# A streaming encoder layer in one planned stream: second home for z tiles, free PSUM positions from one list, state decay as a step of its own

## The chip, the cores and the metric

One Trainium2 chip, one of its cores. The metric is the device time of one execution in microseconds, from launch to end. The profiled execution has besides a span, from its first to its last instruction.

## The reference, cut to what matters

One layer for 2048 prompt rows and 64 sample rows, model width 1024. The input projection has 10,272 columns; a Mamba-2 branch works in chunks over 8 groups of 4 heads, a pooling branch beside it, then two branch projections, a merge and an output projection.

```python
n = rmsnorm(x, norm_g)
z, xbc, dt_raw, u, pool_gate, gate_logits = split(n @ w_in)
xs, bs, cs = split(silu(causal_dwconv(xbc_ext)))
# ssd_chunk, one chunk:
y_diag = einsum('blgsr,bsgrp->blgrp', CB[..., None] * L, xdt)
y_off  = einsum('blgn,bgrpn->blgrp', C, h) * exp(acum)
h_new  = h * exp(acum[:, -1]) + einsum('blgn,blgrp->bgrpn', B, xdt * decay_end)
# behind the scan:
yf = (y + d_skip * xs) * silu(z)
yg = yf * rsqrt(mean(yf * yf, over the 256 columns of a group) + EPS)
out = (sigmoid(g_a) * (yg @ w_branch_ssd) + sigmoid(g_b) * pool_branch) @ w_out
```

## The kernel before, in words

The rows are handled in three parts of 704 (the third has 640 prompt rows and the 64 sample rows). All large products are done in float32 split into a high and a low half, three matmuls for one product, and the input projection uses seven products in place of eight for a pair of 128-column blocks (a Strassen scheme, class `Pair`, products numbered 1 to 7).

The program of a part is a list of items in `Stream`. An item is one product of 12 matmuls (128x352) that reads one weight slot of eight; the slot is split up to five items ahead by ScalarE (high half, L170) and VectorE (low half, L231). `stream.at(position, step)` puts any other step ahead of the item at that position, and `stream.later(k, step)` puts it k items behind the one where it is called. So the position table in `add_part` decides where each step stands on each engine. TensorE, and after the start ScalarE too, run in exactly this program order; VectorE and the DMA queue of SyncE (SP) are ordered by the tile scheduler along it, and each engine runs its own list in order.

The pairs of a part come in this order: u and pool gate, then merge gates `g`, then for each of 8 groups the pairs `x`, `bc` and `z`. While these products run, the scan of the group before is threaded through them, six units to a group (`unit_load`, `unit_mask`, `unit_exp`, `unit_front`, `unit_back`):

- `unit_front` transposes x and B into the PSUM bank `tp` and forms C·B there; VectorE makes `xdt`, `xdtd` and the masked `bA` of it (L847 to L850).
- `unit_back` makes y in bank `y` and the new state in bank `st`. GpSimd (POOL) decays the state `h` in place (L887) once the y matmuls have read it, then VectorE adds the product (L892). `eB` holds the decay of y, loaded by ScalarE's DMA queue.
- In the third part the sixth unit has the sample rows: its state `hsr` is loaded, turned by TensorE in bank `st` and copied to `hs` by ScalarE, all at the head of `unit_front`.
- Behind a group's last unit come `group_post` (times silu(z), then a DMA of the result to `y_d`), `group_square`, and twice `group_sum` (split of half of the sum of squares into `sqr`) and `group_rms` (two matmuls with ones into the bank `e`).

The bank `e` (one buffer) belongs to product 2 of each pair; the list `quiet` has the positions between, where it is free. `zt` and `sa` have one buffer each, for all z tiles but the last and for all merge gate tiles. Each `group_rms` of the second half is followed by a chain: DMA to `s2_d`, DMA back, VectorE, POOL power, DMA to `rs_d`. In the first part the split slots of x, bc and u are also stored to DRAM (L327), and the other parts load them.

Of the kernel before, what the change touches and what calls it, by code (L numbers as in the profile page):

```python
# [19 lines left out]
NG = 8  # L20
# [110 lines left out]
def kernel(  # L131
# [152 lines left out]
    class Pair:  # L284
# [10 lines left out]
        def early(self, i):  # L295

            if self.stored():
                return ()
            return {1: ((9, 1, self.load0),), 6: ((10, 1, self.load1), (7, 0, self.sums)),
                    3: ((12, 0, self.sum4),)}.get(i, ())  # L300

        def load0(self):
            self.r0 = cols(w_in, pair_cols[self.key][0])
# [248 lines left out]
    def add_part(qi, q):  # L552
# [221 lines left out]
        def z_pair(g):  # L774
            st = grp[g]

            def open_(t):
                if "zt" not in st:
                    if g + 1 < NG:
                        st["zt"] = nm["pc"].tile([P, 2, T], F32, tag="zt", name="zt", bufs=1)  # L780
                    else:
                        st["zt"] = nm["pc"].tile([P, 2, XW], F32, tag="xx", name="zt", bufs=4)[:, :, 0:T]
# [42 lines left out]
        def unit_front(u):  # L825
            g, ci = divmod(u, NC)
            kind, r0, lt, L, xp = q.chunks[ci]
            pc, un, st = nm["pc"], units[u], grp[g]
            xx, bc, bA = st["xx"], st["bc"], un["bA"]
            xs = slice(xp, xp + L)  # L830
            if kind == "s":
                hs = st["hs"] = pc.tile([P, 256], F32, tag="hs", name="hs", bufs=1)
                ps = tpsum("st")
                for t in range(2):
                    transpose(ps[:, t * P:(t + 1) * P], st["hsr"][:, t, :], ident)
                S.copy(out=hs, in_=ps[:, 0:256])
# [13 lines left out]
            V.tensor_tensor(out=bA[0:L, :, 0:L], in0=bA[0:L, :, 0:L],  # L850
                            in1=cb.unsqueeze(1).broadcast_to([L, HPG, L]), op=ALU.mult)
# [7 lines left out]
                dma_a(eB[hh * 64:(hh + 1) * 64, :, 0:L], src.unsqueeze(0).broadcast_to([64, 2, L]))  # L859

        def sample_load(g):
            hsr = grp[g]["hsr"] = nm["pc"].tile([P, 2, P], F32, tag="hsr", name="hsr", bufs=1)
            dma(hsr, state_ssd[0, 0, 4 * g:4 * g + 4].rearrange("(t h) p n -> (h p) t n", t=2))

        def unit_back(u):
            g, ci = divmod(u, NC)
# [17 lines left out]
            if kind == "p":  # L884
                sp = tpsum("st")
                mm(sp[:, 0:256], lhsT=un["bt"][0:L], rhs=un["xdtd"][0:L], start=True, stop=True)
            G.tensor_tensor(out=hd(hcur), in0=hd(hcur),  # L887
                            in1=q.dec[:, ci, 4 * g:4 * g + 4].unsqueeze(2).broadcast_to([P, HPG, 64]), op=ALU.mult)
            yv = st["yt"][:, :, lt:lt + L]
            V.tensor_tensor(out=yv, in0=yb[:, 1, :, 0:L], in1=eB[:, :, 0:L], op=ALU.mult)  # L890
            V.tensor_tensor(out=yv, in0=yb[:, 0, :, 0:L], in1=yv, op=ALU.add)
            V.tensor_tensor(out=hcur, in0=sp[:, 0:256], in1=hcur, op=ALU.add)  # L892

        def group_post(g):
            st = grp[g]
            xx, yt, zt = st["xx"], st["yt"], st["zt"]
            for t0, sl, sg in q.segs:
                for j in range(2):
                    V.scalar_tensor_tensor(out=yt[:, j, t0:t0 + sl], in0=xx[:, j, t0 + sg:t0 + sg + sl],
                                           scalar=dcol[:, 2 * g + j:2 * g + j + 1], in1=yt[:, j, t0:t0 + sl],  # L900
                                           op0=ALU.mult, op1=ALU.add)
            V.tensor_tensor(out=yt, in0=yt, in1=zt, op=ALU.mult)
            dma(y_d[g], yt)
            if not q.last:
                dma(h_d[g], st["h"])
# [12 lines left out]
        def group_rms(g, h):  # L918
            pc, zt, sqr = nm["pc"], grp[g]["zt"], grp[g]["sqr"]
            srow = zt[:, 1]  # L920
            ps = bank("e") if g + 1 < NG else any_tpsum()
            for i in range(2):
                mm(ps[0:32, 0:H], lhsT=onesr, rhs=sqr[:, i], start=i == 0, stop=i == 1)
            S.copy(out=srow[0:1, h * H:(h + 1) * H], in_=ps[0:1, 0:H])
            if not h:
                return
            dma(s2_d[g:g + 1], srow[0:1])
            sc4 = pc.tile([P, 16], F32, tag="sc4", name="sc4")[0:64, 0:NB]
            dma(sc4, s2_d[g].rearrange("(p f) -> p f", f=NB))
            V.tensor_scalar(out=sc4, in0=sc4, scalar1=1.0 / 256, scalar2=EPS, op0=ALU.mult, op1=ALU.add)  # L930
            G.tensor_tensor(out=sc4, in0=sc4, in1=mhalf[0:64, 0:NB], op=ALU.pow)
            dma(rs_d[g].rearrange("(p f) -> p f", f=NB), sc4)
# [65 lines left out]
        quiet = sorted([after[n, 6] for n in range(len(pairs))] + [after[n, 5] for n in range(len(pairs))])  # L998
        before = lambda u, x: slots[u - 1] + x * (slots[u] - slots[u - 1]) if u > 0 else slots[0] - 3.5 * (1 - u - x)
        for u in range(NG * NC + 1):  # L1000
            g, ci = divmod(u, NC)
            if u < NG * NC:
# [1 line left out]
                stream.at(before(u, 0.15), lambda u=u: unit_mask(u))  # L1004
                stream.at(before(u, 0.5), lambda u=u: unit_exp(u))
                stream.at(slots[u], lambda u=u: unit_front(u))
                stream.at(before(u + 1, 0.2), lambda u=u: decay_load(u))
                if q.ns and ci == 3:
                    stream.at(slots[u], lambda g=g: sample_load(g))
            if u:  # L1010
                stream.at(slots[u], lambda u=u: unit_back(u - 1))
            if u and ci == 0:
                g -= 1
                p = max(slots[u], ready("z", g) + 1.5) + 0.01
                if g + 1 < NG:
                    r0, r1, t0, t1 = [t for t in quiet if t >= p + 4.4][0:4]
                else:
                    t0, t1, r0, r1 = p + 1.5, p + 3, p + 4.5, p + 6.5
                stream.at(p, lambda g=g: group_post(g))
                stream.at(p + 2, lambda g=g: group_square(g))  # L1020
                stream.at(p + 3.2, lambda g=g: group_sum(g, 0))
                stream.at(r0, lambda g=g: group_rms(g, 0))
                stream.at(r0 + 0.1, lambda g=g: group_sum(g, 1))
                stream.at(r1, lambda g=g: group_rms(g, 1))
                if q.last:
                    stream.at(t0, lambda g=g: group_state(g, grp[g]["hs"], ssd_s, "e3"))
                    stream.at(t1, lambda g=g: group_state(g, grp[g]["h"], ssd_p, "e1"))
# [340 lines left out]
```

## Time and profile before

| | |
|---|---|
| three runs | 3227.84, 3229.19, 3238.91 us; median 3229.19 us |
| profiled execution | 3231.66 us, span 3229.6 us |
| TensorE (PE) busy | 2958.2 us, 92% of the span |
| VectorE (DVE), ScalarE (ACT), GpSimd (POOL) busy | 1961.9, 1467.8, 829.0 us |
| mean granted TensorE clock | 0.955 of full speed |

The profiled execution lies 2.47 us over the median. PE is the engine with least idle time, so what counts is where PE stands still, and at which clock it runs behind that.

### The profile page before, as it was taken

The numbers are of one execution on the slowest core, as the hardware profiler recorded it, in microseconds if no ns is written. First come the engines' busy times: TensorE is split into PE (matmuls) and PEld (weight loads), VectorE is DVE, ScalarE is ACT, GpSimd is POOL, SyncE is SP. The second block draws the span as 40 slices with busy tenths as digits, with TensorE's granted clock in tenths as the row PEclk, the third lists the DMA queues.
The fourth block names the chain that finished last, engine by engine and source line by source line (L and its number), as shares of the span: only waits on it lengthen the run. The fifth ranks groups of instructions, "written<-read, shape, count | busy, mean of one in ns | idle before, by whom it ended". The sixth has DMA issues, their size and how long they took to land.

```text
span 3229.6 us, 50452 instructions
## 1 busy us (share of the span) xinstructions
PE 2958.2 (92%) x18794; PEld 2827.3 (88%) x18794; DVE 1961.9 (61%) x3462; ACT 1467.8 (45%) x2896; POOL 829.0 (26%) x996
## 2 busy tenths in 40 slices
PE   6999898988899999999899889999999889887998
PEld 6998787878899999998888889999998878887998
DVE  7776767776654556665666665365665566665522
ACT  5445555555442433454544543243345545463411
POOL 4344433433200022322332410012232223341000
PEclk9999998889999999999999999999999999998999
DMA  5566665654586655676565466455567655545734
GB/s 174 180 206 180 216 182 180 223 182 112 198 257 215 211 183 183 198 217 180 158 190 151 103 229 206 148 189 168 189 177 219 177 163 167 151 115 189 230 104 147
DMA packets 502057, 585.07 MB, mean 181 GB/s; under 512 B 43461, under 2 KB 399133, under 8 KB 501813
## 3 DMA queue, kind: packets, MB, share of 16 engines
q1 hardware_dynamic: 390453, 531.50, 49.9%
q10 hardware_dynamic: 111360, 50.36, 8.0%
q8 instruction: 148, 2.42, 0.3%
q14 instruction: 96, 0.79, 0.1%
HBM read 434.31 MB, written 147.44 MB: 180 GB/s over the span
## 4 chain that ended last, share of the span: by engine, by line
PE 37%; DVE 7%; DMA 6%; ACT 4%; issue 2%; POOL 1%; ACTq 1%; SPq 0%; DVEq 0%; POOLq 0%
PE ps_a L183 15%; PE ps_d L183 10%; PE ps_e L183 5%; PE ps_y L183 3%; PE ps_st L183 2%; DVE xx L762 1%; DMA y_d<-yt 1%; DMA bA<-ac_d 1%; PE ps_tp L186 1%; PE ps_tp L183 1%; DVE w L231 1%; DMA wraw<-y_d 1%; DMA g_d<-sa 1%; DMA gt<-g_d 1%; ACT xx L174 1%
## 5 line engine op out<-in xcount | busy, mean ns | idle before, releaser
L183 PE MATMUL ps_a<-N,w 128*128 128x352 f32 x5760 | 998.2, 328 | 30.3 <-ACT e L170 26.2
L183 PEld LDWEIGHTS ps_a<-N,w 128*128 128x128 f32 x5760 | 950.2, 192 | 40.3 <-ACT e L170 32.6
L183 PE MATMUL ps_d<-N,w 128*128 128x352 f32 x2880 | 525.5, 340 | 6.8 <-DVE sa L353 6.8
L183 PEld LDWEIGHTS ps_d<-N,w 128*128 128x128 f32 x2880 | 498.5, 201 | 18.5 <-DVE sa L353 7.3
L231 DVE TENSOR_TENSOR w<-wraw,w 128x512 fp32r<-128x512 f32 x544 | 423.3, 793 | 122.8 <-ACT w L170 120.3
L170 ACT CAST w<-wraw 128x512 fp32r<-128x512 f32 x544 | 326.9, 616 | 158.9 <-POOL wraw L180 61.9
L180 POOL TENSOR_TENSOR S<-wraw 128x512 f32<-128x512 f32 x160 | 232.6, 1454 | 328.2 <-DVE w L231 172.7
L170 ACT COPY e<-ps_a 128x352 f32<-128x352 f32 x360 | 160.4, 448 | 286.1 <-PE ps_a L183 253.3
L183 PE MATMUL ps_e<-N,w 128*128 128x352 f32 x1440 | 273.2, 341 | 8.5 <-DVE ue L353 3.3
L183 PEld LDWEIGHTS ps_e<-N,w 128*128 128x128 f32 x1440 | 247.3, 197 | 14.4 <-DVE sa L353 3.7
L180 POOL TENSOR_TENSOR wraw<-wraw 128x512 f32<-128x512 f32 x160 | 234.0, 1462 | 92.2 <-DVE w L231 83.6
L815 POOL TENSOR_SCALAR_AFFINE_SELECT bA<-bA 128x512 f32<-128x512 f32 x144 | 104.8, 728 | 471.0 <-DMA bA<-ac_d 427.0
L174 ACT ACTIVATE bA<-bA,acum 128x128 f32<-128x128 f32 (+1 forms) x576 | 178.7, 381 | 26.6 <-issue 7.6
L762 DVE SCALAR_TENSOR_TENSOR bc<-raw,cwT,bc 128x704 f32<-128x704 f32 (+1 forms) x144 | 150.4, 1044 | 55.5 <-ACT bc L174 53.8
L762 DVE SCALAR_TENSOR_TENSOR xx<-raw,cwT,xx 128x704 f32<-128x704 f32 (+1 forms) x144 | 154.8, 1075 | 40.4 <-ACT xx L174 39.3
L174 ACT ACT_TABLE_LOAD x105 | 134.7, 1283 | 58.3 <-DVE zt L353 40.3
L892 DVE TENSOR_TENSOR h<-ps_st,h 128x256 f32<-128x256 f32 x136 | 57.1, 420 | 162.8 <-POOL h L887 140.4
L231 DVE TENSOR_TENSOR w<-S,w 128x512 fp32r<-128x512 f32 x176 | 122.0, 696 | 47.9 <-ACT w L170 47.9
L417 POOL TENSOR_TENSOR ss<-ss,mhalf 128x1 f32<-128x1 f32 (+1 forms) x18 | 10.7, 598 | 531.9 <-DVE ss L415 531.9
L183 PE MATMUL ps_d<-yn,w 128*128 128x352 f32 x798 | 131.7, 322 | 0.6 <-DVE w L231 0.2
L183 PE MATMUL ps_a<-yn,w 128*128 128x352 f32 x798 | 130.8, 322 | 0.1
L183 PEld LDWEIGHTS ps_d<-yn,w 128*128 128x128 f32 x798 | 127.8, 188 | 1.9 <-DVE w L231 1.3
(334 smaller groups left out, 4754.5 us busy)
## 6 DMA issues: line engine op xcount, KB each, us to landing
wraw<-in_w_in_dram SPq DMA_DIRECT2D x160, 512.0 KB
w<-wc_x SPq DMA_DIRECT2D x112, 512.0 KB
w<-wc_bc SPq DMA_DIRECT2D x112, 512.0 KB
bA<-ac_d ACTq DMA_DIRECT2D x120, 256.0 KB
wc_x<-w SPq DMA_DIRECT2D x56, 512.0 KB
wc_bc<-w SPq DMA_DIRECT2D x56, 512.0 KB
w<-wc_u SPq DMA_DIRECT2D x56, 512.0 KB
wraw<-in_w_branch_ssd_dram SPq DMA_DIRECT2D x48, 512.0 KB
```

The costliest lines, as they stand in the source:

```text
L170: S.pin(nc.scalar.copy(**k))
L174: S.pin(nc.scalar.activation(*a, **k))
L180: tc.keep_in_program_order(G.tensor_tensor(**k))
L183: tc.keep_in_program_order(nc.tensor.matmul(*a, **k))
L186: tc.keep_in_program_order(nc.tensor.transpose(*a))
L231: V.tensor_tensor(out=dst_lo, in0=src, in1=dst_hi.bitcast(F32), op=ALU.subtract)
L417: G.tensor_tensor(out=ss[0:L, 2:3], in0=ss[0:L, 1:2], in1=mhalf[0:L, 0:1], op=ALU.pow)
L762: V.scalar_tensor_tensor(out=xx[:, i, 0:XL], in0=raw[:, t:t + XL], scalar=cwT[:, t, ct:ct + 1], in1=xx[:, i, 0:XL], op0=ALU.mult, op1=ALU.add)
L815: G.affine_select(out=bA[0:L, :, 0:L], in_=bA[0:L, :, 0:L], compare_op=ALU.is_ge, fill=-1e30, base=0, pattern=[[0, HPG], [1, L]], channel_ ...
L892: V.tensor_tensor(out=hcur, in0=sp[:, 0:256], in1=hcur, op=ALU.add)
```

## The change

- `z` tiles take turns between two homes: even groups in `zt`, odd groups in the merge gates' tile `sa`, the last group as before. The pair of merge gate 3 moves from group 4 to group 5, so that no z tile and gate meet in `sa`. Where two gate pairs follow each other (the last three), the first finishes (products 4 and 3) before product 2 of the next.
- `group_post` writes its product into `zt` itself, the DMA to `y_d` reads `zt`, and `group_square` squares `zt` in place.
- All uses of bank `e` between products draw from one list (`free_bank` takes a position out). The two halves of the mean square now have their `group_sum` two items or more ahead of `group_rms`, and 4 to 7 items between the halves.
- The decayed state is formed ahead by `unit_decay` into a tile `hd`, pinned in POOL's order; `unit_back` only adds.
- The sample state is loaded into a buffer of `eB` and turned by its own step `sample_turn`, in bank `e`.
- Units start one item later (7 for 6 behind the bc pair), the last group's six units take 15 items for 18, `decay_load` comes 0.6 of a unit earlier, `group_square` one item later.
- DMAs of the chain behind the mean square, of `y_d`, `h_d` and of the weight store are issued some items later.

```diff
             if wd is not None:
-                dma(wd[:, i - 1], flat_slot(s))
+                stream.later(2, lambda: dma(wd[:, i - 1], flat_slot(s)))
...
+                    if g + 1 == NG:
+                        st["zt"] = nm["pc"].tile([P, 2, XW], F32, tag="xx", name="zt", bufs=4)[:, :, 0:T]
+                    elif g % 2:
+                        st["zt"] = nm["sg"].tile([P, 2, T], F32, tag="sa", name="zt", bufs=1)
+                    else:
                         st["zt"] = nm["pc"].tile([P, 2, T], F32, tag="zt", name="zt", bufs=1)
...
-            if kind == "s":
-                hs = st["hs"] = pc.tile([P, 256], F32, tag="hs", name="hs", bufs=1)
-                ps = tpsum("st")
-                for t in range(2):
-                    transpose(ps[:, t * P:(t + 1) * P], st["hsr"][:, t, :], ident)
-                S.copy(out=hs, in_=ps[:, 0:256])
...
+        def unit_decay(u):
+            g, ci = divmod(u, NC)
+            h = grp[g]["h" if q.chunks[ci][0] == "p" else "hs"]
+            t = units[u]["hd"] = nm["pc"].tile([P, 256], F32, tag="hd", name="hd", bufs=1)
+            tc.keep_in_program_order(G.tensor_tensor(
+                out=hd(t), in0=hd(h), in1=q.dec[:, ci, 4 * g:4 * g + 4].unsqueeze(2).broadcast_to([P, HPG, 64]),
+                op=ALU.mult))
...
+        def sample_turn(g):
...
+            ps = bank("e") if g + 1 < NG else any_tpsum()
...
-            G.tensor_tensor(out=hd(hcur), in0=hd(hcur),
-                            in1=q.dec[:, ci, 4 * g:4 * g + 4].unsqueeze(2).broadcast_to([P, HPG, 64]), op=ALU.mult)
...
-            V.tensor_tensor(out=hcur, in0=sp[:, 0:256], in1=hcur, op=ALU.add)
+            V.tensor_tensor(out=hcur, in0=sp[:, 0:256], in1=un["hd"], op=ALU.add)
...
-            V.tensor_tensor(out=yt, in0=yt, in1=zt, op=ALU.mult)
-            dma(y_d[g], yt)
+            V.tensor_tensor(out=zt, in0=yt, in1=zt, op=ALU.mult)
+            stream.later(1.5, lambda: dma(y_d[g], zt))
...
-            S.activation(zt, grp[g]["yt"], AF.Square)
+            S.activation(zt, zt, AF.Square)
...
+            stream.later(1, lambda: dma(s2_d[g:g + 1], srow[0:1]))
+            stream.later(2.5, lambda: dma(sc4, s2_d[g].rearrange("(p f) -> p f", f=NB)))
+            stream.later(4, power)
+            stream.later(6, lambda: dma(rs_d[g].rearrange("(p f) -> p f", f=NB), sc4))
...
-            seq += [(n, 6), (n - 1, 3), (n, 5), (n, 7), (n + 1, 1), (n + 1, 2), (n, 4)]
+            seq += [(n, 6), (n - 1, 3), (n, 5), (n, 7), (n + 1, 1)]
+            same = n + 1 < len(pairs) and pairs[n].key[0] == pairs[n + 1].key[0] == "g"
+            seq += [(n, 4), (n, 3), (n + 1, 2)] if same else [(n + 1, 2), (n, 4)]
...
-        S0 = [ready("bc", g) + 6 for g in range(NG)]
-        S0.append(S0[-1] + 18)
+        S0 = [ready("bc", g) + 7 for g in range(NG)]
+        S0.append(S0[-1] + 15)
...
-                stream.at(before(u + 1, 0.2), lambda u=u: decay_load(u))
+                t = before(u, 0.6)
...
+                stream.at(before(u + 1, 0.45), lambda u=u: unit_decay(u))
...
-                    r0, r1, t0, t1 = [t for t in quiet if t >= p + 4.4][0:4]
+                    r0 = free_bank(p + (6 if g in (3, 5, 6) else 10))
+                    r1 = free_bank(r0 + 4)
...
-                stream.at(p + 2, lambda g=g: group_square(g))
-                stream.at(p + 3.2, lambda g=g: group_sum(g, 0))
+                stream.at(p + 3, lambda g=g: group_square(g))
+                stream.at(r0 - 2, lambda g=g: group_sum(g, 0))
```

What this moves, at three places. First ScalarE behind the z pair of group 0 in the first part, before: the square (`zt<-yt`), the split of the first half (`sqr`), and the copy that takes its sum out of bank `e` (`zt<-ps_e`).

```order
L170 CAST w<-S 128x512
L174 ACTIVATE zt<-yt 128x1408
L170 COPY bt<-ps_tp 128x128
L170 CAST w<-wraw 128x512
L170 COPY sa<-ps_a 128x11x32
L177 DMA eB<-eac_d 64x2x128 x2
L170 CAST sqr<-zt 128x352
L170 CAST w<-wraw 128x512
L170 COPY e_3319<-ps_a 128x352
L177 DMA bA<-ac_d 128x4x128
L170 COPY zt<-ps_e 1x352
```

The same queue in the change; the square (`zt<-zt`) stands 13 rows ahead of the first of these rows, directly behind `sa<-ps_a`.

```order
L170 COPY bt<-ps_tp 128x128
L170 CAST w<-S 128x512
L170 CAST sqr<-zt 128x352
L170 CAST w<-wraw 128x512
L170 COPY raw<-ps_a 128x11x32
L174 ACTIVATE xx<-raw,colT,cwT 128x704
L177 DMA bA<-ac_d 128x4x128
L174 ACTIVATE bA<-bA,acum 128x128 x4
L170 CAST w<-wraw 128x512
L170 COPY e_3516<-ps_a 128x352
L177 DMA eB<-eac_d 64x2x128 x2
L170 COPY zt<-ps_e 1x352
```

The square has moved behind the copy out of `ps_a`, and between the split and the copy out of `ps_e` stand eight rows where three stood.

Second TensorE at the sample unit of group 0 in the third part, before: the turn of the sample state (`hsr`) in bank `st`, and the matmul that needs this bank again.

```order
L183 MATMUL ps_d<-N,w 128x352 x24
L183 MATMUL ps_a<-N,w 128x352 x24
L186 MATMUL ps_st<-ident,hsr 128x128 x2
L186 MATMUL ps_tp<-ident,xx 64x128 x2
L186 MATMUL ps_tp<-ident,bc 64x128
L183 MATMUL ps_tp<-bc 64x64
L183 MATMUL ps_y<-bA,xdt 64x128 x4
L183 MATMUL ps_y<-bc,h 128x128 x2
L183 MATMUL ps_st<-xdtd,bt 128x256
```

And in the change:

```order
L183 MATMUL ps_d<-N,w 128x352 x12
L186 MATMUL ps_e<-ident,hsr 128x128 x2
L183 MATMUL ps_a<-N,w 128x352 x24
L183 MATMUL ps_e<-N,w 128x352 x12
L186 MATMUL ps_tp<-ident,xx 64x128 x2
L186 MATMUL ps_tp<-ident,bc 64x128
L183 MATMUL ps_tp<-bc 64x64
L183 MATMUL ps_y<-bA,xdt 64x128 x4
L183 MATMUL ps_y<-bc,h 128x128 x2
L183 MATMUL ps_st<-xdtd,bt 128x256
```

The turn has left bank `st` for bank `e`, whose next user is product 2, two products on (`x24` are two products).

Third POOL in the first part, where units of group 1 run, before: the sums for the weight factors (`S`, `wraw`), the mask of a unit (`bA`) and the decay of the state in place.

```order
L180 TENSOR_TENSOR wraw<-wraw 128x512
L887 TENSOR_TENSOR h<-h,dec 128x256
L815 AFFINE_SELECT bA<-bA 128x512
L180 TENSOR_TENSOR S<-wraw 128x512
L887 TENSOR_TENSOR h<-h,dec 128x256
L764 COPY hcar<-raw 128x3
```

And in the change:

```order
L180 TENSOR_TENSOR wraw<-wraw 128x512 x2
L817 AFFINE_SELECT bA<-bA 128x512
L866 TENSOR_TENSOR hd<-h,dec 128x256
L180 TENSOR_TENSOR S<-wraw 128x512
L764 COPY hcar<-raw 128x3
L817 AFFINE_SELECT bA<-bA 128x512
```

The decay is still one instruction for each unit, but it reads `h` and writes `hd`, so it waits for the state before it and no longer for the matmuls that read it.

## Rows read from the trace of the kernel before

**Rows 1.** The page, section 1: busy us, share of the span, instructions of each engine

```profile
PE 2958.2 (92%) x18794; PEld 2827.3 (88%) x18794; DVE 1961.9 (61%) x3462; ACT 1467.8 (45%) x2896; POOL 829.0 (26%) x996
```

**Rows 2.** Busy us by stretch: PE, PEld, DVE, ACT, POOL; granted clock; DMA share, GB/s

```profile
240.00:860.00 620.00, 541.36 (x3315) 503.48 (x3314) 432.72 (x726) 341.14 (x675) 256.12 (x272) 0.92 0.58 180
860.00:1340.00 480.00, 466.89 (x3046) 458.89 (x3045) 266.21 (x476) 187.08 (x362) 51.15 (x66) 0.99 0.67 217
1340.00:1880.00 540.00, 496.46 (x3164) 462.13 (x3163) 350.17 (x604) 279.18 (x558) 175.52 (x210) 0.95 0.55 164
...
2390.00:2950.00 560.00, 493.19 (x3116) 462.05 (x3114) 345.37 (x638) 283.90 (x580) 175.74 (x250) 0.93 0.55 161
```

**Rows 3.** PE's waits over the span: total us, times, longest us

```profile
PE ps_e L183 <- DVE sqr L231: 42.4, 31, 3.2
PE ps_e L183 <- ACT sqr L170: 29.6, 20, 5.6
PE ps_tp L186 <- ACT bc L174: 27.1, 13, 4.0
...
PE ps_st L183 <- ACT hs L170: 25.1, 5, 6.1
PE ps_tp L186 <- DVE bA L850: 17.0, 9, 4.7
PE ps_y L183 <- DVE yt L891: 12.0, 5, 4.3
PE ps_st L183 <- ACT sqr L170: 8.2, 2, 7.7
```

**Rows 4.** Timeline of PE behind group 0 of part one: start, duration, idle before

```profile
334.99 0.35 PE L183 MATMUL ps_e<-sqr,onesr 128*32 128x352 f32 x1 [2.17 <-ACT sqr L170]
338.17 0.50 PE L183 MATMUL ps_e<-sqr,onesr 128*32 128x352 f32 x1 [2.83 <-DVE sqr L231]
338.47 6.31 PE L183 MATMUL ps_d<-N,w 128*128 128x352 f32 x24
...
352.89 3.98 PE L183 MATMUL ps_a<-N,w 128*128 128x352 f32 x24
```

**Rows 5.** Line 887, the state's decay: ns min/median/max; who waited for it

```profile
L887 POOL TENSOR_TENSOR h<-h,dec x136: 605/615/2086, 271.0 to 2897.9; 128x256 f32<-128x256 f32 x136
...
DVE h L892: 140.4, 57
```

**Rows 6.** A DVE split beside POOL's sums (timeline), and all such splits (line 231)

```profile
337.82 3.13 POOL L180 TENSOR_TENSOR wraw<-wraw 128x512 f32<-128x512 f32 x2
338.04 1.76 DVE L231 TENSOR_TENSOR w<-wraw,w 128x512 fp32r<-128x512 f32 x1
...
L231 DVE TENSOR_TENSOR w<-wraw,w x544: 627/685/2855, 14.9 to 3124.3; 128x512 fp32r<-128x512 f32 x182
```

**Rows 7.** Timeline behind group 0: issue to y_d, the square, the next copies on ACT

```profile
328.35 0.32 SPq L903 DMA_DIRECT2D y_d<-yt  x1
...
331.00 1.38 ACT L174 ACTIVATE zt<-yt 128x1408 f32<-128x1408 f32 x1
...
332.95 0.45 ACT L170 COPY sa<-ps_a 128x352 f32<-128x352 f32 x1
```

**Rows 8.** Timeline, end of part one: a 704 KB DMA out of sa, the next write

```profile
835.94 0.53 SPq L794 DMA_DIRECT2D g_d<-sa  x1
...
841.78 0.53 DVE L353 TENSOR_TENSOR sa<-ps_e,e 128x352 f32<-128x352 f32 x1 [0.97 <-DMA g_d<-sa]
```

**Rows 9.** Waits of the DMA queue on SP over the span: total us, times, longest

```profile
SPq L255 <- DVE w L231: 367.9, 102, 16.4
...
SPq L927 <- ACT zt L170: 143.1, 22, 15.8
```

**Rows 10.** Timeline, end of part three: gate tile, then the ones matmul on PE

```profile
2922.12 0.53 DVE L353 TENSOR_TENSOR sa<-ps_e,e 128x352 f32<-128x352 f32 x1 [6.26 <-DMA g_d<-sa]
...
2923.57 1.06 PE L183 MATMUL ps_st<-sqr,onesr 128*32 128x352 f32 x2 [7.65 <-ACT sqr L170]
```

More of the change, by code (lines that the diff above doesn't have):

```diff
@@ L299, in early @@
             return {1: ((9, 1, self.load0),), 6: ((10, 1, self.load1), (7, 0, self.sums)),
-                    3: ((12, 0, self.sum4),)}.get(i, ())
+                    3: ((12 - (self.key == ("g", NG - 1)), 0, self.sum4),)}.get(i, ())
         def load0(self):
@@ L778, in open_ @@
                 if "zt" not in st:
-                    if g + 1 < NG:
+                    if g + 1 == NG:
[3 more added lines that the diff above has]
+                    else:
                         st["zt"] = nm["pc"].tile([P, 2, T], F32, tag="zt", name="zt", bufs=1)
-                    else:
-                        st["zt"] = nm["pc"].tile([P, 2, XW], F32, tag="xx", name="zt", bufs=4)[:, :, 0:T]
                 return st["zt"][:, t], 0, 0
@@ L861, in sample_load @@
         def sample_load(g):
-            hsr = grp[g]["hsr"] = nm["pc"].tile([P, 2, P], F32, tag="hsr", name="hsr", bufs=1)
+            hsr = grp[g]["hsr"] = nm["pc"].tile([P, 2, P], F32, tag="eB", name="hsr")
             dma(hsr, state_ssd[0, 0, 4 * g:4 * g + 4].rearrange("(t h) p n -> (h p) t n", t=2))
+        def unit_decay(u):
[6 more added lines that the diff above has]
+        def sample_turn(g):
+            st = grp[g]
+            hs = st["hs"] = nm["pc"].tile([P, 256], F32, tag="hs", name="hs", bufs=1)
+            ps = bank("e") if g + 1 < NG else any_tpsum()
+            for t in range(2):
+                transpose(ps[:, t * P:(t + 1) * P], st["hsr"][:, t, :], ident)
+            S.copy(out=hs, in_=ps[:, 0:256])
         def unit_back(u):
@@ L901, in group_post @@
                                            op0=ALU.mult, op1=ALU.add)
-            V.tensor_tensor(out=yt, in0=yt, in1=zt, op=ALU.mult)
-            dma(y_d[g], yt)
+            V.tensor_tensor(out=zt, in0=yt, in1=zt, op=ALU.mult)
+            stream.later(1.5, lambda: dma(y_d[g], zt))
             if not q.last:
-                dma(h_d[g], st["h"])
+                stream.later(1, lambda: dma(h_d[g], st["h"]))
         def group_square(g):
             zt = grp[g]["zt"]
-            S.activation(zt, grp[g]["yt"], AF.Square)
+            S.activation(zt, zt, AF.Square)
             V.tensor_tensor(out=zt[:, 0], in0=zt[:, 0], in1=zt[:, 1], op=ALU.add)
@@ L926, in group_rms, with power @@
                 return
-            dma(s2_d[g:g + 1], srow[0:1])
             sc4 = pc.tile([P, 16], F32, tag="sc4", name="sc4")[0:64, 0:NB]
[L929 to L932, printed above, removed]
+            def power():
+                V.tensor_scalar(out=sc4, in0=sc4, scalar1=1.0 / 256, scalar2=EPS, op0=ALU.mult, op1=ALU.add)
+                tc.keep_in_program_order(G.tensor_tensor(out=sc4, in0=sc4, in1=mhalf[0:64, 0:NB], op=ALU.pow))
+            stream.later(1, lambda: dma(s2_d[g:g + 1], srow[0:1]))
+            stream.later(2.5, lambda: dma(sc4, s2_d[g].rearrange("(p f) -> p f", f=NB)))
+            stream.later(4, power)
+            stream.later(6, lambda: dma(rs_d[g].rearrange("(p f) -> p f", f=NB), sc4))
         def group_state(g, src, dst, tag):
@@ L956, in add_part @@
         for g in range(NG):
-            if g in (1, 4):
+            if g in (1, 5):
                 put(("g", 2 + g // 4), gate_pair(2 + g // 4))
@@ L969, in add_part @@
         for n in range(len(pairs)):
-            seq += [(n, 6), (n - 1, 3), (n, 5), (n, 7), (n + 1, 1), (n + 1, 2), (n, 4)]
+            seq += [(n, 6), (n - 1, 3), (n, 5), (n, 7), (n + 1, 1)]
+            same = n + 1 < len(pairs) and pairs[n].key[0] == pairs[n + 1].key[0] == "g"
+            seq += [(n, 4), (n, 3), (n + 1, 2)] if same else [(n + 1, 2), (n, 4)]
         seq = [(n, i) for n, i in seq + [(len(pairs) - 1, 3)] if 0 <= n < len(pairs)]
+        seq = list(dict.fromkeys(seq))
         after, pools_due = {}, []
@@ L993, in add_part, with free_bank @@
             stream.at(ready("bc", g) + 4, lambda g=g: conv_silu(g, "bc"))
-        S0 = [ready("bc", g) + 6 for g in range(NG)]
-        S0.append(S0[-1] + 18)
+        S0 = [ready("bc", g) + 7 for g in range(NG)]
+        S0.append(S0[-1] + 15)
         slots = [S0[g] + (S0[g + 1] - S0[g]) * k / NC for g in range(NG) for k in range(NC)] + [S0[-1]]
         quiet = sorted([after[n, 6] for n in range(len(pairs))] + [after[n, 5] for n in range(len(pairs))])
+        def free_bank(t):
+            t = [i for i in quiet if i >= t][0]
+            quiet.remove(t)
+            return t
         before = lambda u, x: slots[u - 1] + x * (slots[u] - slots[u - 1]) if u > 0 else slots[0] - 3.5 * (1 - u - x)
@@ L1006, in add_part @@
                 stream.at(slots[u], lambda u=u: unit_front(u))
-                stream.at(before(u + 1, 0.2), lambda u=u: decay_load(u))
-                if q.ns and ci == 3:
-                    stream.at(slots[u], lambda g=g: sample_load(g))
+                t = before(u, 0.6)
+                if q.ns and ci > 3:
+                    t = before(u + 1, 0.1) if ci == 4 else before(u, 0.6)
+                stream.at(t, lambda u=u: decay_load(u))
+                stream.at(before(u + 1, 0.45), lambda u=u: unit_decay(u))
+                if q.ns and ci == 3:
+                    stream.at(before(u + 1, 0.3), lambda g=g: sample_load(g))
+                    t = slots[u] + 4
+                    if g + 1 < NG:
+                        t = free_bank([i for i in quiet if i <= slots[u + 2] + 1][-1])
+                        assert t > slots[u] + 2.5
+                    stream.at(t, lambda g=g: sample_turn(g))
             if u:
@@ L1015, in add_part @@
                 if g + 1 < NG:
-                    r0, r1, t0, t1 = [t for t in quiet if t >= p + 4.4][0:4]
+                    if q.last:
+                        t0, t1 = free_bank(slots[u] + 0.5), free_bank(p + 0.5)
+                    r0 = free_bank(p + (6 if g in (3, 5, 6) else 10))
+                    r1 = free_bank(r0 + 4)
                 else:
-                    t0, t1, r0, r1 = p + 1.5, p + 3, p + 4.5, p + 6.5
+                    t0, t1, r0, r1 = p + 1.5, p + 3, p + 6, p + 7.5
                 stream.at(p, lambda g=g: group_post(g))
-                stream.at(p + 2, lambda g=g: group_square(g))
-                stream.at(p + 3.2, lambda g=g: group_sum(g, 0))
+                stream.at(p + 3, lambda g=g: group_square(g))
+                stream.at(r0 - 2, lambda g=g: group_sum(g, 0))
                 stream.at(r0, lambda g=g: group_rms(g, 0))
@@ L1025, in add_part @@
                 if q.last:
-                    stream.at(t0, lambda g=g: group_state(g, grp[g]["hs"], ssd_s, "e3"))
-                    stream.at(t1, lambda g=g: group_state(g, grp[g]["h"], ssd_p, "e1"))
+                    stream.at(t0, lambda g=g: group_state(g, grp[g]["h"], ssd_p, "e1"))
+                    stream.at(t1, lambda g=g: group_state(g, grp[g]["hs"], ssd_s, "e3"))
                 post_end = r1 + 1
```

## The prediction

> **What bounds the kernel now.** I read the page's first section first: PE is busy 92% of the span, the next engine, DVE, 61% [rows 1]. So time can only be won where PE stands still or runs at a low clock. Busy time by stretch says where that is. In the three stretches in which the scan runs between the products, PE is busy 541.36 of 620 us, 496.46 of 540 and 493.19 of 560; in the stretch between the first two, 466.89 of 480 [rows 2]. Idle in the three: 78.6 + 43.5 + 66.8 = 188.9 us. The clock falls there too: its mean is 0.92, 0.95 and 0.93, against 0.99 outside [rows 2]. Of a stretch of T us at mean clock c, T x (1 - c) is lost work: 49.6 + 27.0 + 39.2 = 115.8 us. The two go together. Behind two waits of 2.17 and 2.83 us, 24 matmuls took 6.31 us, where 24 undisturbed ones took 3.98 [rows 4]; matmuls at the lower level (1.2 for 2.4 GHz) explain that. So I price one us of PE idle at 1 + 115.8/188.9 = 1.61 us of time.
>
> Then PE's waits say for whom it stands still [rows 3]. The largest is the mean square: the ones matmuls wait for `sqr`, 42.4 + 29.6 + 8.2 = 80.2 us. Then B's silu on ACT 27.1 us, the copy of the sample state `hs` 25.1, the bank `tp` that DVE has not read yet (`bA`) 17.0, and bank `y`, likewise, 12.0. Together 161.4 of the 188.9. These are waits for engines that are late, not for busy ones: DVE is busy 70% of the first stretch (432.72 of 620) and 62 to 65% of the others, ACT 51 to 55% [rows 2].
>
> **The change, part by part.** Mean square. Before, a half is split one item ahead of its matmuls, and the second half is split just behind the first one's matmuls. An item is 12 matmuls, 3.98/2 = 1.99 us [rows 4]. Now four groups of eight have two items between split and matmul, five between square and split, and seven between the halves: I take all of their half of the 80.2, 40.1 us. Three groups (3, 5, 6) have two items, one more than before, and five between the halves: the second half's wait goes, of the first's (two waits of at most 5.0 us together in [rows 4]) two us; I take three quarters of 30.1, 22.6. The last group gains almost nothing: 0 of 10. Sum 62.7 us, bounds 0 and 80.2.
>
> Sample state. The turn now stands three products ahead of the sample unit's front, in a bank that no matmul needs for two products, 4 us. The copy on ACT has that time. I take 22 of 25.1 us; bounds 0 and 25.1. What could be late next is the load of `hsr`, issued three items ahead: 6 us and a unit, against 5.8 us for a DMA five times as large (a tile from issue at 835.94 to the write that waited for it at 841.78) [rows 8].
>
> Units one item later. B's silu gets 1.99 us more; 13 waits of 2.1 us on average, 4.0 at most [rows 3], are between nearly gone and half left. I take half, 14 us; bounds 0 and 13 x 1.99 = 25.9.
>
> Decayed state. DVE's add waited 140.4 us for POOL, which waited for PE's read of the state and stood behind its sums [rows 5]. Now POOL may start when the state before is there, half a unit ahead. That frees DVE, not PE; PE gets it through `bA` and `y`, 17.0 + 12.0 = 29.0 us, between 0 and 29.0. I take a third, 10 us, since ACT's share in these waits stays.
>
> Together 62.7 + 22 + 14 + 10 = 109 us of PE idle (bounds 0 and 80.2 + 25.1 + 25.9 + 29.0 = 160).
>
> What it adds. The square now overwrites what the DMA to `y_d` reads, and waits for it on ACT. Behind it on ACT stand the splits and the copies out of bank `a`, and PE waits for those. From [rows 7]: the DMA was issued at 328.35; a DMA of the same size took 5.8 us [rows 8], so it lands at 334.2; the square's new place, behind the copy out of `ps_a`, is reached at 332.95 + 0.45 = 333.4. So ACT waits 0.8 us at 24 places. PE needs the next copy out of bank `a` three products later, 6.0 us, so it should see nothing; for other groups, where ACT may be earlier, I take 0.5 us each, 12 us (bounds 0 and 24 x 5.8 = 139). The decay runs on POOL at 0.615 us for a unit as before [rows 5]; where POOL is blocked at a mask and `hd` comes late, the old wait is back: 10 us, between 0 and the 29 above. `eB` shares two buffers with `hsr`, and z tiles share `sa` with gates: a handful of waits for a release, 6 us, bounds 0 and the 6.26 us that DVE stood at such a tile once in each part's tail [rows 10], thrice, 19. Together 28 us.
>
> At nothing: the later DMA issues. SP stood blocked at the chain's first DMA for 143.1 us, and at loads behind splits for 367.9 [rows 9], yet no row of PE's waits names a weight load: the eight slots cover it. If that cover were gone, the blocked SP would be the price, and the change makes it shorter. The order of the last gate pairs may shorten the tail in which ACT and PE stood 7.65 us behind one gate tile [rows 10]; I count nothing, as the DMA stays.
>
> Net 109 - 28 = 81 us, times 1.61 = 130 us. From the profiled execution's 3231.66: 3101; it lies 2.5 us over the median, so **3099 us**.
>
> **A rule against it.** A split on DVE, 685 ns in the median, took 1.76 us while POOL's sums ran [rows 6]. Before the change POOL decays while DVE stands and waits for it; afterwards the 144 decays (3 parts of 8 groups of 6 units) run beside a working DVE, 144 x 0.615 = 88.6 us. If each holds DVE up for its whole length, DVE gets back 140.4 - 88.6 = 52 us, and rival two says what the time is then. The Trainium skill, page "SBUF — State Buffer", sections "SBUF: two separate sides" and "Who interferes with whom", has the two engines share a port pair under an exclusive lock: a DVE instruction with two SBUF inputs and a GpSimd one exclude each other, and the loser blocks wholly. The split of [rows 6] agrees with that rule; by it rival two's time would come out, by the sum above 3099 us.
>
> **Rivals.** One, DVE was the root. If DVE's 140.4 us are what makes `bA`, `y`, B's silu and part of `sqr` late, all 161.4 us of waits go but 20: 141 x 1.61 = 227 us, **3002**. For it: the largest single row ends with DVE. Against: ACT ends 90 of the 161.4 us [rows 3], and each in-order queue meets its next wait.
>
> Two, POOL and DVE collide. DVE's own gain shrinks to 52/140 of what I took; units and decayed state give 24 x 0.37 = 9 instead of 24: 15 x 1.61 = 24 us less, **3123**. For it [rows 6]; against: POOL also collided before, with everything but this op.
>
> Three, the waits move. PE arrives earlier at ACT and DVE, whose work stays; half of the 109 us comes back as waits for copies and splits: 54 - 28 = 26, times 1.61 = 42 us, **3187**. For it: DVE at 70% in the first stretch. Against: 30% free.
>
> Four, slower: the square behind a late DMA. SP runs in order; if a load ahead of the `y_d` DMA blocks SP for b us, ACT stands 0.8 + b us at the square, and PE is covered for 6.0 - 1.38 (the square) - 0.45 = 4.2 us [rows 7]; it loses b - 3.4 at each of 24 groups. The gain of 109 - 16 = 93 us (the other new waits taken off) is used up at 93/24 + 3.4 = 7.3 us. SP's waits at such loads are 3.6 us on average, 16.4 at most [rows 9]. At b = 10: 24 x 6.6 = 158, net -65, times 1.61: **3334**. Against: before, the same DMA stood behind the same loads and was issued as soon as its data was there.
>
> Five, no change: b near 7, or all of the 109 us back: **3229**.
>
> **How the numbers follow.** Chances: forecast 0.48, one 0.17, two 0.12, three 0.10, four 0.07, five 0.06. A measurement of this kernel tells about 0.5%, 16 us, from no change. Faster by more than that: 0.87; within: 0.06; slower: 0.07. The predicted time is the likeliest case's, 3100. The range of 8 in 10 takes in rivals two and three and most of one, and leaves out four, five and the lower part of one: 3010 to 3200. The likeliest case alone: 3060 to 3140.
>
> **What would show it.** Right: the waits for `sqr` under 20 us, for `hs` under 5, no row in which DVE waits long for POOL at the state's add, and mean clocks of 0.95 or more in all three stretches. Square: a wait of ACT for a DMA at `zt`, below 30 us in all, and PE's waits for copies out of bank `a` not larger than before. Wrong: PE's waits for `e` copies or splits grow by as much as `sqr` loses (three); DVE's splits lengthen (two); ACT waits over 150 us at the square (four). The clock is the weak term: half of it hangs on the waits left being few and short.

## The result and the profile after

The kernel after takes 3025.35 us (median of four, 3021.56 to 3031.44), the kernel before, beside it, 3231.85 us: a ratio of 0.9361 with a 95% interval of 0.9337 to 0.9384. The direction was forecast, the size was not: 130 us were expected, 206 came.

The page of the kernel after, first section (busy us, share of the span, instructions), answers to [rows 1]:

```profile
span 3019.8 us, 50603 instructions
## 1 busy us (share of the span) xinstructions
PE 2869.6 (95%) x18794; PEld 2760.6 (91%) x18794; DVE 2004.7 (66%) x3462; ACT 1464.7 (49%) x2896; POOL 883.2 (29%) x996
```

PE idle is 3019.8 - 2869.6 = 150.2 us; before, it was 3229.6 - 2958.2 = 271.4. So 121.2 us of the 209.8 us of span came out of idle time. The other 88.6 came out of PE's busy time, with the same 18,794 matmuls: they ran at a higher clock. Busy time by stretch shows it, for the three scan stretches (which lie earlier now) and the two between them; the columns are those of [rows 2]:

```profile
240.00:860.00 620.00, 570.92 (x3673) 537.51 (x3673) 502.53 (x799) 368.42 (x722) 286.06 (x272) 0.97 0.68 209
860.00:1280.00 420.00, 411.92 (x2716) 405.29 (x2715) 223.36 (x408) 159.85 (x320) 51.85 (x67) 0.99 0.64 210
1280.00:1820.00 540.00, 525.11 (x3491) 499.54 (x3490) 396.26 (x668) 306.80 (x597) 189.12 (x209) 1.00 0.65 194
1820.00:2230.00 410.00, 401.88 (x2662) 395.50 (x2661) 216.88 (x419) 148.44 (x302) 58.38 (x91) 1.00 0.57 181
2230.00:2730.00 500.00, 485.52 (x3274) 460.73 (x3273) 369.37 (x664) 290.07 (x605) 199.25 (x265) 0.99 0.64 186
```

The clock, 0.92 to 0.95 in the scan before, is 0.97, 1.00 and 0.99. What PE still waits for, in all, answers to [rows 3] (line and bank, who is waited for, us in total, times, longest):

```profile
PE ps_a L183 <- ACT e L170: 30.0, 13, 6.3
PE ps_tp L186 <- DVE bA L846: 22.3, 17, 3.3
PE ps_e L183 <- DVE sqr L231: 10.9, 6, 2.5
...
PE ps_e L183 <- ACT sqr L170: 3.2, 1, 3.2
...
PE ps_tp L183 <- ACT sqr L170: 2.9, 1, 2.9
```

With a row of 0.4 the waits for `sqr` are 17.4 us, where they were some 80; those for `hs` and for B's silu are gone. `bA` has risen from 17.0, and bank `a`, waiting for ScalarE's copies, from this row of before:

```profile
PE ps_a L183 <- ACT e L170: 26.2, 14, 5.7
```

Two rows of the other engines, VectorE's add behind POOL's decay ([rows 5]) and ScalarE's square behind the DMA to `y_d`:

```profile
DVE h L903 <- POOL hd L866: 30.5, 18, 3.7
```

```profile
ACT zt L174 <- DMA y_d<-zt: 52.3, 12, 6.5
```

From the waits alone one would say that the mean square gave its 62.7 us of idle exactly as forecast, and that the rest was under-sized. The runs say otherwise.

### The profile page after: what moved, and what is told of

Read it like the earlier page. It is cut to its first block, busy times and chain, and to the rows that moved or that the text cites. A ratio compares the mean times of both kernels' runs of the same rounds, so it can differ in the third digit from the quotient of the medians.

```text
span 3019.8 us, 50603 instructions
## 1 busy us (share of the span) xinstructions
PE 2869.6 (95%) x18794; PEld 2760.6 (91%) x18794; DVE 2004.7 (66%) x3462; ACT 1464.7 (49%) x2896; POOL 883.2 (29%) x996
## 5 line engine op out<-in xcount | busy, mean ns | idle before, releaser
L183 PEld LDWEIGHTS ps_a<-N,w 128*128 128x128 f32 x5760 | 946.2, 191 | 43.8 <-ACT e L170 35.7
L231 DVE TENSOR_TENSOR w<-wraw,w 128x512 fp32r<-128x512 f32 x544 | 436.1, 817 | 114.4 <-ACT w L170 112.2
L183 PE MATMUL ps_d<-N,w 128*128 128x352 f32 x2880 | 504.7, 327 | 1.2 <-DVE zt L353 1.2
L183 PEld LDWEIGHTS ps_d<-N,w 128*128 128x128 f32 x2880 | 469.1, 189 | 10.1 <-issue 4.6
L180 POOL TENSOR_TENSOR wraw<-wraw 128x512 f32<-128x512 f32 x160 | 246.1, 1538 | 88.8 <-DVE w L231 77.8
L183 PE MATMUL ps_e<-N,w 128*128 128x352 f32 x1440 | 258.8, 329 | 5.0 <-DVE ue L353 3.3
L183 PEld LDWEIGHTS ps_e<-N,w 128*128 128x128 f32 x1440 | 239.0, 192 | 6.6 <-DVE ue L353 3.6
L762 DVE SCALAR_TENSOR_TENSOR xx<-raw,cwT,xx 128x704 f32<-128x704 f32 (+1 forms) x144 | 168.8, 1172 | 33.4 <-ACT xx L174 32.1
L762 DVE SCALAR_TENSOR_TENSOR bc<-raw,cwT,bc 128x704 f32<-128x704 f32 (+1 forms) x144 | 158.2, 1098 | 35.8 <-ACT bc L174 34.6
L183 PEld LDWEIGHTS ps_a<-yn,w 128*128 128x128 f32 x798 | 128.1, 188 | 1.9 <-ACT w L170 1.4
```

The costliest lines, as they stand in the source:

```text
L180: tc.keep_in_program_order(G.tensor_tensor(**k))
L183: tc.keep_in_program_order(nc.tensor.matmul(*a, **k))
L231: V.tensor_tensor(out=dst_lo, in0=src, in1=dst_hi.bitcast(F32), op=ALU.subtract)
L762: V.scalar_tensor_tensor(out=xx[:, i, 0:XL], in0=raw[:, t:t + XL], scalar=cwT[:, t, ct:ct + 1], in1=xx[:, i, 0:XL], op0=ALU.mult, op1=ALU.add)
```

## The experiments

Two theories went in. By the **terms theory** each stall of PE belongs to the part of the change that was aimed at it. By the **root theory** (rival one) VectorE's 140.4 us behind POOL were the root of most stalls, and the decay formed ahead gave most of the gain. Four runs undo one part each; times are to be held against 3025.

**1. Decay in place again.**

```diff
+G.tensor_tensor(out=hd(hcur), in0=hd(hcur),
+                in1=q.dec[:, ci, 4 * g:4 * g + 4].unsqueeze(2).broadcast_to([P, HPG, 64]), op=ALU.mult)
...
-V.tensor_tensor(out=hcur, in0=sp[:, 0:256], in1=un["hd"], op=ALU.add)
+V.tensor_tensor(out=hcur, in0=sp[:, 0:256], in1=hcur, op=ALU.add)
...
-stream.at(before(u + 1, 0.45), lambda u=u: unit_decay(u))
```

> The kernel after, with the decay put back where the kernel before had it: POOL multiplies the state in place inside unit_back, and VectorE's add takes the product in the state's own tile; no unit_decay, all else as after. The terms theory (each stall of TensorE goes with its own part of the change; the decay ahead is worth 10 us of idle, 16 us of time): 3030 to 3050 us, and the stalls for the mean square (sqr) and for B's silu (bc) stay below 25 us together. The root theory (what VectorE lost at the state's add, 140.4 us before and 30.5 us after, made it late for everything behind it): VectorE's wait for POOL at the add comes back to over 110 us, and with it half or more of the sqr, bc and y waits of TensorE: 3080 us or more.

3078.48 us, ratio 0.9517 (0.9498 to 0.9535): 53 us lost, far above the terms theory's 3030 to 3050 and 1.5 us short of where the root theory begins. Busy times, VectorE's wait at the add, and PE's largest waits in this kernel:

```profile
PE 2890.0 (94%) x18794; PEld 2776.3 (90%) x18794; DVE 1969.3 (64%) x3462; ACT 1465.1 (48%) x2896; POOL 841.0 (27%) x996
```

```profile
DVE h L905 <- POOL h L900: 171.3, 91, 6.9
```

```profile
PE ps_tp L186 <- DVE bA L846: 36.0, 23, 5.4
PE ps_a L183 <- ACT e L170: 32.2, 14, 7.5
PE ps_e L183 <- DVE sqr L231: 17.9, 6, 3.7
PE ps_e L183 <- DVE w L231: 9.3, 6, 3.4
```

VectorE stood 141 us longer at the add, and PE 35.5 us longer in all (3075.7 - 2890.0 = 185.7 idle), over many rows: `bA` 14, `sqr` 10 over all its rows (17.4 to 27.0), and the wait for weight splits `w` at bank `e` rose from 1.7 to 9.3. The time alone would not decide, the rows do: `sqr` is far from its 80.2 of before, and the waits for `hs` and B's silu did not come back, so VectorE was not the root of these. But the part is worth three times the 16 us forecast.

**2. Mean square late.**

```diff
-r0 = free_bank(p + (6 if g in (3, 5, 6) else 10))
-r1 = free_bank(r0 + 4)
+r0 = free_bank(p + 4.4)
+r1 = free_bank(r0 + 1)
...
-stream.at(r0 - 2, lambda g=g: group_sum(g, 0))
+stream.at(max(p + 3.2, r0 - 1.2), lambda g=g: group_sum(g, 0))
```

> The kernel after, with the mean square of a group at the distances of before: the first split 1.2 items ahead of its matmuls, and the two parts at the first two free places from 4.4 items behind group_post. All else as after, the decay ahead too. Terms theory: the sqr waits of TensorE come back to some 80 us, 62.7 idle us at 1.6 is 100 us: 3100 to 3130 us. Root theory: VectorE, no longer held at the add, makes the splits in time from there too: under 40 us of sqr waits, 3030 to 3065 us.

3112.52 us, 0.9622 (0.9601 to 0.9643): 87 us, as the terms theory had it. But ScalarE, not VectorE, ended most of it: this kernel's PE waits have

```profile
PE ps_e L183 <- ACT sqr L170: 84.0, 20, 9.1
```

where before had 29.6; all rows for `sqr` make 109.6. The square was left at three items, just ahead of the split, and behind its DMA. Run 10 mends that.

**3. Sample turn in `unit_front`,** in bank `st`; the load, and the free place of bank `e` taken out of the list, are left as in after:

```diff
+hs = st["hs"] = pc.tile([P, 256], F32, tag="hs", name="hs", bufs=1)
+ps = tpsum("st")   # two transposes of hsr, S.copy to hs: at the head of unit_front
...
-stream.at(t, lambda g=g: sample_turn(g))
```

> The kernel after, with the sample state turned inside the last unit_front again, through a bank st, and ScalarE's copy right behind the two transposes; it is still loaded into the ring of eB at the place that after gives it. Terms theory: TensorE waits for hs 25 us again, as before; 3045 to 3070 us. Root theory: the wait is ScalarE's and has nothing to do with VectorE, so it comes back too, but as ScalarE has less to wait for now, perhaps half of it: 3035 to 3055 us.

3063.51 us, 0.947 (0.9453 to 0.9487): 38 us; PE waits 18.7 us for `hs` again. The forecast had 22 x 1.61 = 35.

**4. Units one item earlier.**

```diff
-S0 = [ready("bc", g) + 7 for g in range(NG)]
-S0.append(S0[-1] + 15)
+S0 = [ready("bc", g) + 6 for g in range(NG)]
+S0.append(S0[-1] + 16)
```

> The kernel after, with the first unit of each group six items behind its B and C pair, as before, and not seven (the last group's span one item longer in return, so that the end of the units stays). Terms theory: B's silu is late again, the bc waits of TensorE come back to 20 to 30 us: 3050 to 3070 us. Root theory: VectorE's evictions of the B and C pair are in time now, so the silu is: bc under 10 us, 3025 to 3040 us.

3066.11 us, 0.9477 (0.9452 to 0.9502): 41 us, the terms theory's side. The waits of PE in this kernel:

```profile
PE ps_a L183 <- ACT e L170: 45.7, 21, 7.2
PE ps_tp L186 <- ACT bc L174: 19.7, 12, 3.8
```

B's silu is late again although VectorE is hardly held at the add (9.3 us); the copies out of bank `a` come later too, and of the 22.3 us for `bA` 2.0 are left.

**5. All four undone,** as in runs 1 to 4.

> The kernel after, with the four undone together that were undone one by one: decay in place, split and matmuls of the mean square at the distances of before, the sample turn in the last unit_front, units one item earlier. What stays of the change: the z tiles' two homes, the order of the gates, the list of free places, the ring of eB, the DMAs issued later. One by one the four cost 53, 87, 38 and 41 us, 219 together. If they are independent (the terms theory): 3225 to 3260 us, and the rest of the change is worth nothing, or costs a little. If they stand in for each other (one engine's lateness pays for two of the stalls): 3130 to 3200 us, and the rest of the change is worth the difference to before's 3232.

3256.85 us, 1.0058 (1.0038 to 1.0077) of before: the four, 219 us one by one, add up to 231. They are nearly independent. That the result lies above before came from the place of run 2's square and its DMA, as run 11 shows.

**6. Decay ahead alone,** the other way round: the kernel before with the edit of run 1 reversed, and `hsr` in the ring of `eB`.

```diff
+stream.at(before(u + 1, 0.45), lambda u=u: unit_decay(u))
...
+V.tensor_tensor(out=hcur, in0=sp[:, 0:256], in1=un["hd"], op=ALU.add)
```

> The kernel before, with the decay formed ahead alone: unit_decay into a tile of its own, pinned on POOL, at the place of after, and the add in unit_back from there. To make room for that tile the sample state is loaded into the ring of eB; nothing else changes. Independent terms: it gives what taking it out of after cost, 53 us: 3165 to 3195 us, with VectorE's wait for POOL at the add under 50 us. Rival, the stalls of the mean square, the sample turn and B's silu swallow it: 3210 to 3235 us, though the wait for POOL goes all the same.

3182.02 us against 3236.49, 0.9828 (0.9803 to 0.9853): 54 us, the same as taking it out of after cost. Its PE waits:

```profile
PE ps_e L183 <- DVE sqr L231: 41.0, 31, 3.8
PE ps_a L183 <- ACT e L170: 40.1, 21, 5.7
PE ps_tp L186 <- ACT bc L174: 23.5, 9, 4.0
PE ps_e L183 <- ACT sqr L170: 21.2, 19, 2.7
PE ps_st L183 <- ACT hs L170: 21.2, 5, 5.3
...
PE ps_tp L186 <- DVE bA L850: 3.6, 5, 1.4
```

Against [rows 3], `bA` loses 13.4 us, `sqr`, `y`, `bc` and `hs` some 4 to 10 each, and bank `a` gains 13.9 on its 26.2. The large stalls stay: the root theory falls.

**7 and 8. The square behind its DMA.** Run 7 gives it more room, run 8 less.

```diff
-stream.at(p + 3, lambda g=g: group_square(g))
+stream.at(p + (3.5 if g in (3, 5, 6, 7) else 6), lambda g=g: group_square(g))   # run 7
...
-stream.later(1.5, lambda: dma(y_d[g], zt))
+stream.later(2.5, lambda: dma(y_d[g], zt))   # run 8
```

> The kernel after, with the square three items later in the four groups that have the room (groups 0, 1, 2 and 4: six items behind group_post, still two ahead of the first split) and half an item later in the others. It asks what ScalarE's wait of 52.3 us for the DMA to y_d costs. If TensorE is covered there: the wait falls by half or more and the time stays, 3018 to 3032 us. If TensorE pays for it behind bank a (its 30.0 us of waits for e copies there): those fall by 10 us or more, and the time by 15 to 40 us.

> The kernel after, with the DMA to y_d issued one item (some 2 us) later, the square where it is: ScalarE's wait at the square doubles, from 52.3 to about 100 us. By the cover of 4.2 us in the prediction, waits of 4.4 us on average that become 6.4 cost TensorE 2 us at each of 12 to 24 places: 24 to 48 us of idle at 1.6, 3060 to 3100 us. If TensorE's slack behind the square is longer than that: 3022 to 3035 us.

ScalarE's wait for the DMA in run 7, then in run 8:

```profile
ACT zt L174 <- DMA y_d<-zt: 13.0, 6, 4.7
```

```profile
ACT zt L174 <- DMA y_d<-zt: 64.0, 12, 8.0
```

Run 7: 3027.95 us, 0.9359 (0.9329 to 0.9388): the wait fell by 39 us and the time stayed, so the 52.3 us are covered. Run 8: 3038.22 us, 0.9379 (0.935 to 0.9409). The wait rose only to 64.0, not to the 100 expected, and PE's for bank `a` from 30.0 to 37.9. The 13 us are less than the 16 us taken as the least that can be told from no change, but all four times of run 8 (3033.82 and up) lie above all four of after (3031.44 at most): a longer wait may begin to cost.

**9. y in its own tile again,** a candidate for a better version too.

```diff
-V.tensor_tensor(out=zt, in0=yt, in1=zt, op=ALU.mult)
-stream.later(1.5, lambda: dma(y_d[g], zt))
+V.tensor_tensor(out=yt, in0=yt, in1=zt, op=ALU.mult)
+dma(y_d[g], yt)
...
-S.activation(zt, zt, AF.Square)
+S.activation(zt, grp[g]["yt"], AF.Square)   # at p + 2
```

> The kernel after, with y gated in its own tile as before: the DMA to y_d reads yt and is issued at once, the square reads yt and writes zt, two items behind group_post as before. So ScalarE has no DMA to wait for at the square (the 52.3 us go to 0); in return the next group's first write to yt waits for the DMA. The run with the square three items later says that this wait costs nothing: 3018 to 3035 us. If it was only moved there and is paid in both: 3000 to 3015 us.

3022.64 us, 0.9347 (0.9331 to 0.9363): no wait of ScalarE for the DMA, and no change that can be told from after.

**10. Mean square at the distances of before,** on run 9: run 2's `r0` and `r1`, `group_sum` at p + 3.2.

> The same (y in its own tile), and the mean square at exactly the distances of before: square 2 items, first split 3.2 items behind group_post, the two parts at the first two free places from 4.4 items on. The first run with a late split left the square at 3 items, 0.2 ahead of the split, and ScalarE ended 84.0 us of the waits for sqr, against 29.6 + 8.2 before; so that run may have undone more than the change did. If so, the sqr waits come to 40 to 75 us here and the time to 3060 to 3095 us; if the distance of the square does not matter, to over 95 us, and 3100 to 3120 us.

3051.37 us, 0.9431 (0.9415 to 0.9446): 29 us, less than any theory had. PE's waits for `sqr`:

```profile
PE ps_e L183 <- DVE sqr L231: 28.8, 13, 4.4
PE ps_e L183 <- ACT sqr L170: 21.1, 9, 5.6
...
PE ps_tp L183 <- ACT sqr L170: 1.7, 1, 1.7
```

With smaller rows they are 51.8 us, against 17.4 in run 9, 34.4 more; but PE's idle rose only from 149.1 to 166.1 us. Bank `y` (11.5 to 5.3), bank `a` (25.6 to 20.5) and `bA` (16.9 to 14.6) gave 13.6 us of it back. Only 2.2 of the 51.8 us fall behind 2050 us, so these 29 us are those of parts one and two. Run 2 cost 58 us more than this one: there the split stood 0.2 items behind the square, and the square behind its DMA. The two were not told apart.

**11. All four undone, on run 10.**

> Decay in place, the sample turn in the last unit_front, units one item earlier, and the mean square and y as in the run before this one. The decay, the turn and the units cost 53, 38 and 41 us one by one. If the four are independent, the time is 3157 us plus what the late split alone costs against y in its own tile (40 to 90 us): 3200 to 3245 us, and near the kernel before, so the rest of the change is worth under 20 us. If the 3257 us of the first such run had another cause than the square's place: 3250 us or more again.

3197.16 us, 0.9887 (0.9859 to 0.9915): above run 9 by 174.5 us, where the single costs (53, 38, 41, 29) make 161. It is still 38.5 us under before, more than I expected of what is left of the change. Where these are, the turns of `hsr` on PE tell, one pair a group of part three. Before, the first and the last:

```profile
L186 PE MATMUL ps_st<-ident,hsr x2: 272/300/328, 2406.8 to 2407.0; 128*128 128x128 f32 x2
...
L186 PE MATMUL ps_st<-ident,hsr x2: 271/272/272, 2895.8 to 2895.9; 128*128 128x128 f32 x2
```

Run 11, the same two:

```profile
L186 PE MATMUL ps_st<-ident,hsr x2: 273/300/328, 2405.6 to 2405.8; 128*128 128x128 f32 x2
...
L186 PE MATMUL ps_st<-ident,hsr x2: 270/270/271, 2862.7 to 2862.8; 128*128 128x128 f32 x2
```

Level at the first, 33 us apart at the last: the net gain is all in part three. There, from 2050 to 3000 us, PE's waits for `sqr` were 13.8, 7.7 and 5.2 us before; in run 11 one is left:

```profile
PE ps_st L183 <- ACT sqr L170: 5.0, 1, 5.0
```

In part three the list hands the first free places to the states' turns, and the mean square gets later ones; my undoing left that as it was. So the mean square is worth some 29 us in parts one and two and, by this reading, up to 32 in part three. The 32 were not tried by themselves, and they are not its alone: `sqr` lost 21.7 us of wait there, but the waits for `hs` lost 8.4 (25.1 to 16.7) and one of 6.8 for a gate tile `sa` went too:

```profile
PE ps_d L183 <- DVE sa L353: 6.8, 1, 6.8
```

Nor is run 11 the kernel before in parts one and two, though level in time: `sqr` stands there at 74.2 us, against 55.3 before. What stays of the change in run 11 (the two homes of z, the order of the gates, the later DMAs, the earlier loads of `eB` and the places in the last group among it) was never undone by itself; whether it gives something stays open.

**12. Units half an item later still,** 7.5 and 14.5 in run 4's lines.

> The kernel after, with the units of each group half an item later still (7.5 behind the B and C pair, the last group's span shorter by half an item). The bc waits are gone already, so the term that gave 41 us has nothing left: 3020 to 3040 us. If ScalarE's copies out of bank a (30.0 us of TensorE's waits) and VectorE's product in bA (22.3 us) come late because the units stand too near behind the silu, both fall: 3000 to 3015 us.

3070.49 us, 0.9491 (0.9475 to 0.9507): 45 us slower, which no theory had. PE's waits:

```profile
PE ps_tp L186 <- DVE bA L846: 50.0, 24, 6.1
PE ps_a L183 <- ACT e L170: 25.0, 12, 6.5
```

Of the three places tried seven is the best: one item less costs 41 us at B's silu and bank `a`, half an item more costs 45 at `bA`. VectorE's own waits for bank `y`, 35.7 us in after, are longer here, but as long in run 4, where `bA` cost PE 2.0 us; here, then in run 4:

```profile
DVE yt L901 <- PE ps_y L183: 93.2, 45, 4.6
```

```profile
DVE yt L901 <- PE ps_y L183: 98.4, 42, 8.0
```

So they do not explain the 50.0 us; why VectorE is late with `bA` stays open. No version beat the kernel after.

## Why the prediction was right, and where its sizes failed

The mechanism held: steps moved on other engines took idle time from PE, and its clock rose with that. The sizes of the parts did not, and they erred both ways: the mean square was forecast at 101 us and gave 61 at most, all the rest together at 29 us and gave 145 or more. That the sum fell only 76 us short is in part luck.

**The price.** 1.61 us of time per us of PE idle held: 209.8 / 121.2 = 1.73 for the whole; and for runs 1 to 4, span against idle, 55.9/35.5, 96.0/63.2, 42.2/28.4 and 45.8/24.1, which is 1.49 to 1.90.

**The parts,** us of time; forecast terms times 1.61:

| | forecast | measured |
|---|---|---|
| mean square | 101 | 29 (run 10), and at most some 32 in part three, not tried by itself |
| sample state | 35 | 38 (run 3) |
| units one item later | 23 | 41 (run 4) |
| decayed state | 16, less 16 for a late `hd` | 53 (run 1), 54 (run 6) |
| square behind its DMA | -19 | 0 (runs 7 and 9) |
| releases | -10 | not seen by themselves |
| together | 130 | 206; the parts make 193 at most |

The other 13 us are what run 11 costs beyond its four parts one by one: they help each other, or run 11 undoes more than the change did. No run tells which.

**Mean square: the term was over-sized.** The step that failed is "I take all of their half of the 80.2". The row of waits did shrink by 63 us, but not through this edit alone. In run 11 `sqr` stands at 79.2 us; with decay, turn and units as in after, and the mean square as it was (run 10), at 51.8. And of the 34.4 us that the edit takes from `sqr` between runs 10 and 9, 13.6 come back at the banks `a` and `y` and at `bA`: rival three's mechanism, here inside one term.

**Decayed state: under-sized.** "I take a third, 10 us" counted only the rows `bA` and `y` for it. Run 6 gives 28.6 us of idle (271.4 to 242.8). `bA` and `y` give 18.1; the waits for `sqr`, B's silu and `hs`, which the term left out, give another 17, and bank `a` takes 13.9 back. The 10 us set aside for a late `hd` did not show: VectorE's wait at the add only fell, from 140.4 to 30.5 us.

**Units: under-sized.** Half of the wait for B's silu was taken, all of it went. Against run 4, bank `a` costs PE 15.7 us less as well, and `bA` 20.3 more.

**The square's DMA: the wait came, the cost did not.** ScalarE waits 52.3 us, more than the 24 x 0.8 = 19 and the 30 that I gave as a sign, yet runs 7 and 9 show no cost. The other sign, bank `a` no larger than before, missed by little: 26.2 to 30.0 us.

**Rivals.** One was nearest in time (3002) by another mechanism: the decay alone gives 54 of the 206 us. Two is there in small. POOL's decay took 713 ns on average before, 675 in run 1 and 847 in after:

```profile
L866 POOL TENSOR_TENSOR hd<-h,dec 128x256 f32<-128x256 f32 x136 | 115.2, 847 | 23.3 <-DVE h L903 21.4 <-DMA wraw<-in_w_in_dram 1.2
```

VectorE was busy 2004.7 us in after and 1969.3 in run 1, with the same 3462 instructions: 35 us, not the 88.6 that rival two reckoned with, and the part still gains 53. The Trainium skill, page "SBUF — State Buffer", section "SBUF: two separate sides", has a VectorE instruction with two inputs in SBUF and a GpSimd one that reads SBUF exclude each other at their shared port pair, the later one standing still until the other ends. By that rule either engine can lose time where they overlap, and the traces agree in direction: both are slower in after than in run 1. How the loss is shared they do not settle: in run 6 the same move left the decay at 721 ns, against 713, while VectorE was busy 26.8 us longer (1961.9 to 1988.7). Three fell as a whole, four by ScalarE's longest wait of 6.5 us, five by the time.

## What to carry to other kernels

A row of waits says where a stall ends, not which edit ends it: work that is late on one engine is paid for at the next place where PE happens to look. Price an edit by the engine time that it frees or delays, and undo parts one at a time; here, twice, four such prices came within 14 us of what the four cost together. An undo must restore every distance: a square left one item too late, behind a DMA, made one of them look three times as dear (87 us for 29).

## What the runs showed of the hardware that I had not expected

The clock repaid nearly three quarters as much as the idle time (88.6 against 121.2 us): PE's busy time fell at the same matmul count, with the mean granted clock going from 0.955 to 0.983. And 52.3 us of waiting on ScalarE, the engine that feeds PE its copies and splits, cost nothing that the chip could show (run 7: 13.0 us of wait, and no change in time that can be told).
